# Layer A's first projections in a written order on three engines

## The chip, the cores and the metric

The kernel runs on one core of a Trainium2 chip. The core has a matrix engine (TensorE, PE in the profile), a vector engine (VectorE, DVE), a scalar engine for activations (ScalarE, ACT), a general engine (GpSimd, POOL) and a queue engine (SyncE, SP); sixteen DMA engines move data between HBM and the on-chip memories. Each engine takes its instructions in the order in which the compiled program lists them and waits, where it must, on semaphores. The metric is the device time of one execution in microseconds (us); the median of several executions is given.

## The reference, cut to what matters

The program is a two-layer decoder trunk over 1024 tokens of width 1024: layer A with sparse attention (compressed blocks, selected blocks, a sliding window), layer B with dilated attention, each followed by a feed-forward part. The change lies in the first steps of layer A:

```
h    = rmsnorm(x, norm_mix[0])
proj = h @ w_in                                  # (1024, 2608)
q, kc, vc, ks, vs, kwn, vwn, gl = split(proj)    # 1024, then six of 256, then 48 gates
k_cmp = gelu(blocks(kc) + pe_k @ w1_k) @ w2_k    # compressed keys; the same for v
bias  = rel_bias[t5_bucket(distance)]            # added to every attention logit
```

All products are to float32 accuracy. The kernel splits both factors into a high and a low part of a reduced type and takes three products for each pair (high x high, high x low, low x high).

## The kernel before

The function `trunk` writes out the whole program. The first stage of layer A, inside `with ExitStack() as c:` from line 567, does the following.

*Normed tokens, turned.* `norm_to_hT` (lines 388 to 402) loads token tiles of 128 x 1024 (`nx`, four buffers), takes the row scale (`row_scale`: square with a sum and square root on ACT, reciprocal on VectorE), scales the rows (`nxn`, line 395), turns 128 x 128 squares on PE against an identity (line 400) and splits the result into `hH` (ACT, line 351) and `hL` (VectorE, line 352), eight tiles each of 128 x 1024 tokens. It is called for token tiles 0 and 1, then 2 and 3, then 4 to 7. The products themselves are issued by `mm3`, lines 375 to 377.

*Compressed-key columns.* `proj_T` multiplies two weight column blocks (128 columns each, `blocks_weights`) with groups of tokens. `evac_c` copies the result into `kc2` by ACT (line 577) and, shifted by one token, by VectorE (lines 579 and 581).

*Bias rows.* `bias_rows` (lines 451 to 463) multiplies the bias table `rb` (33 x 16) with a onehot matrix (33 x 1917) in four products of up to 512 columns (line 461), copies them to `R` (line 462) and stores `R` to memory as `sR`. Later, `bias_skewed` copies it eight times, two heads at a time, with 128 shifted rows, into `sA` (line 472), from where the attention reads its bias. Each copy is issued by SP behind the newest weight load at that place.

*Values and gates.* `tok_proj` (line 418) with 304 columns gives the window values and the gates: for each of the eight token tiles, 24 products. `evac_v` (line 668) splits the values into `vt` (two buffers), stores them from POOL (line 672) and copies the gates (line 674).

*Behind it* come the compression, the second values, the compressed-value columns and the keys and queries, all with the same helpers, up to the attention, whose order is planned by the class `Order`.

Weights come through the class `Weights`: three raw buffers (`wraw`), five high (`wh`) and five low ones (`wl`), used in turn; a load is one DMA of SP and one split. Six PSUM banks named `mm` are shared by transposes, bias products, block columns and values, in the order in which the program asks for them.

What sets the order: except in the attention parts, where `Order` links instructions by hand, a compile-time scheduler lists the instructions of each engine; it takes the program's order as priority and, by a simulated time line, lets a later instruction go first where an earlier one isn't ready. SP's DMA issues are ordered in the same way. In the trace the values' weight splits, for example, stand between the norms and the splits of the first tokens.

Of the kernel before, what the change touches and what calls it, by code (L numbers as in the profile page):

```python
# [11 lines left out]
F32 = mybir.dt.float32  # L12
# [9 lines left out]
D = 1024  # L22
NT = S // 128
KC = D // 128
H = 16
# [89 lines left out]
class Order:  # L115
# [88 lines left out]
    def done(self):  # L204
# [75 lines left out]
        queued = mybir.DependencyInfo(mybir.DependencyClass.NoSync, mybir.DependencyReason.DATA)  # L280
        for e, row in order.items():
            if e == "SP":
                continue
            for a, b in zip(row, row[1:]):
                self.tc.add_manual_dep(b, a.name, queued, reason="order")
# [14 lines left out]
def trunk(ctx, tc, I, out):  # L300
# [33 lines left out]
    nc.vector.memset(eps, 1e-6)  # L334

    def gain(name, ap):
        t = cst.tile([128, KC], F32, name=name)
        nc.gpsimd.dma_start(t, ap.rearrange("(k p) -> p k", p=128))
# [15 lines left out]
    class Weights:  # L354
# [6 lines left out]
        def load(self, src, a, n, gains=None):  # L361
            raw, wh, wl = (r.tile() for r in self.rings)
            v = lambda t: t[:, :a * n].rearrange("p (a n) -> p a n", n=n)
            self.last = nc.sync.dma_start(v(raw), src.rearrange("(a p) n -> p a n", p=128))
            if gains is not None:
                nc.gpsimd.tensor_mul(v(raw), v(raw), gains.unsqueeze(2).to_broadcast([128, a, n]))
            split(wh[:, :a * n], wl[:, :a * n], raw[:, :a * n])
            return v(wh), v(wl)
# [19 lines left out]
    def norm_to_hT(p, xget, gains, hH, hL, t0, n):  # L388

        xs = []  # L390
        for t in range(t0, t0 + n):
            xt = xget(t)
            xn = p.tile([128, D], F32, name="nxn", bufs=4)
            rs = row_scale(p, xt, xn)
            nc.vector.tensor_scalar(xn, xt, rs, None, op0=OP.mult)
            xs.append(xn)
        for k in range(KC):
            pt = bank("mm")
            for i in range(n):
                nc.tensor.transpose(pt[:, i * 128:(i + 1) * 128], xs[i][:, k * 128:(k + 1) * 128], ident)  # L400
            tk = slice(t0 * 128, (t0 + n) * 128)
            split(hH[k][:, tk], hL[k][:, tk], pt[:, :n * 128], gains[:, k:k + 1])
# [15 lines left out]
    def tok_proj(ws, n, hT, tokens, evac):  # L418

        hH, hL = hT  # L420
        for t in range(NT):
# [29 lines left out]
    def bias_rows(p):  # L451
        rb = p.tile([33, H], F32, name="rb")
        nc.vector.memset(rb, 1.0)
        nc.gpsimd.dma_start(rb[0:32], I["rel_bias"])
        R = p.tile([H, NL], F32, name="R")
        for lo in range(0, NL, 512):
            n = min(512, NL - lo)
            oh = p.tile([33, 512], F32, name="oh", bufs=2)
            nc.gpsimd.dma_start(oh[:, :n], I["onehot"][:, lo:lo + n])
            ps = bank("mm")  # L460
            nc.tensor.matmul(ps[:H, :n], rb, oh[:, :n], start=True, stop=True)
            nc.vector.tensor_copy(R[:, lo:lo + n], ps[:H, :n])
        nc.gpsimd.dma_start(sR, R)
# [103 lines left out]
    with ExitStack() as c:  # L567
        wts = Weights([(pool(c, "pw", "right"), (3, 5, 5))])
        cctx = ExitStack()
# [22 lines left out]

        with ExitStack() as c2:
# [8 lines left out]
            kc2, ws = None, []  # L602
            for t0, n in ((0, 2), (2, 2), (4, 4)):
                norm_to_hT(np_, xget, g_mix[0], *hT, t0, n)
                if t0 < 4:
                    ws.append(blocks_weights(0, len(ws)))
                if t0 == 0:
                    kc2 = blocks_tile()
                done = t0 * 128, (t0 + n) * 128
                if t0 == 2:  # L610
                    proj_T(ws[0], hT, evac_c(kc2, 0), (done,))
                    proj_T(ws[1], hT, evac_c(kc2, 1), ((0, 512),))
                else:
                    for ch in range(len(ws)):
                        proj_T(ws[ch], hT, evac_c(kc2, ch), (done,))
        cp = pool(cctx, "pc")
        st = pool(c, "pst", "right")
# [50 lines left out]
        def evac_v(i):  # L668
            def f(t, ps):
                vt = st.tile([128, G, 128], F32R, name="vt", bufs=2)  # L670
                split(vt[:, :, 0:64], vt[:, :, 64:128], ps[:, :256].rearrange("p (g d) -> p g d", d=64))
                nc.gpsimd.dma_start(vS[i, t], f32(vt))
                if i == 1:
                    nc.vector.tensor_copy(gates[:, t, :], ps[:, 256:304])
            return f

        bias_rows(cp)
        tok_proj(wide(wts, W[:, 2304:2608], 304, 3), 304, hT, natural, evac_v(1))
# [24 lines left out]
        def store_blockind():  # L703
            for a in range(2):
                cols = slice(a * 512, (a + 1) * 512)
                raw = st.tile([16, 512], F32, name="bif", bufs=1)
                nc.gpsimd.dma_start(raw, I["blockind"][:, cols])
                t = st.tile([128, 512], F32R, name="sth", bufs=2)
# [1260 lines left out]
```

## Time and profile before

| | us |
|---|---|
| median of 3 runs | 2913.47 |
| lowest, highest | 2911.92, 2920.52 |
| the profiled execution | 2908.86 |
| its span in the profile | 2907.1 |
| first instruction of PE | 8.14 |
| last product of the values and gates ends | 86.44, where the first product of the compression follows |

The profile comes from one execution. Its span runs from the first to the last instruction; 1.8 us of the execution's time lie around it. Times in the text are from the span's start. A line such as "L400" is a line of the kernel before. In a group of instructions "x12" counts them, and "[3.35 <-DVE hL L352]" is idle time of the engine ahead of it, with what ended it. "PEclk" is the share of TensorE's full clock that was granted.

### The profile page before, as it was taken

What the parts mean: (1) busy time and instruction counts of PE and PEld (TensorE: products, weight loads), DVE (VectorE), ACT (ScalarE), POOL (GpSimd) and SP (SyncE); (2) the same over time, 40 slices, a digit from 0 to 9 for tenths busy, and PEclk for the clock granted to TensorE, in tenths of its full rate; (3) what the DMA queues carried; (4) which work ended last, traced back from release to release, by engine and by line L of the source; (5) the groups of instructions that cost most, each with busy time, mean ns of one, the idle gap of its engine ahead of it and who ended that gap; (6) DMA issues with size and microseconds to landing.
All of it is one profiled execution on the core that took longest, in us unless ns stands there. A gap on an engine that the chain in (4) does not pass through costs nothing.

```text
span 2907.1 us, 43848 instructions
## 1 busy us (share of the span) xinstructions
PE 2817.1 (97%) x14766; PEld 2371.2 (82%) x14766; DVE 2260.1 (78%) x4465; ACT 1522.0 (52%) x3314; POOL 1541.3 (53%) x1776
## 2 busy tenths in 40 slices
PE   7999999999999999999999999899999999999997
PEld 6988899898878888888777788788877788888885
DVE  5441999997488888988876776698965888888887
ACT  5431888886443333333554444689855433333334
POOL 2134877873165555555447786455522655555551
PEclk9999999999999999999999999999999999999999
DMA  6756243203122322231225555976421211111112
GB/s 167 232 159 190 64 111 89 62 24 117 30 70 68 80 62 66 66 80 51 92 86 161 150 161 159 281 200 187 135 88 37 75 60 52 55 54 59 52 44 76
DMA packets 266833, 294.46 MB, mean 101 GB/s; under 512 B 18099, under 2 KB 209475, under 8 KB 266608
## 3 DMA queue, kind: packets, MB, share of 16 engines
q1 hardware_dynamic: 246960, 231.50, 27.4%
q0 software_dynamic: 19648, 60.16, 6.8%
q8 instruction: 117, 1.92, 0.3%
q14 instruction: 108, 0.88, 0.1%
HBM read 228.49 MB, written 78.81 MB: 106 GB/s over the span
## 4 chain that ended last, share of the span: by engine, by line
PE 70%; DVE 16%; ACT 4%; issue 4%; DMA 3%; POOL 3%; SPq 1%; DVEq 0%; ACTq 0%; POOLq 0%
PE ux L375 5%; PE ux L376 5%; PE ux L377 5%; PE pt L485 5%; DVE pl L1003 5%; PE uy L375 4%; PE uy L376 4%; DVE xr L1061 4%; PE uy L377 4%; PE dx L376 3%; PE dx L377 3%; PE dr L375 3%; PE dx L375 3%; PE mm L375 3%; PE dr L376 3%
## 5 line engine op out<-in xcount | busy, mean ns | idle before, releaser
L1003 DVE TENSOR_TENSOR pl<-oT,ph 128x512 fp32r<-128x512 f32 x325 | 324.1, 1018 | 71.2 <-ACT ph L1002 61.9
L1002 ACT ACTIVATE ph<-oT 128x512 fp32r<-128x512 f32 x325 | 196.3, 626 | 214.0 <-PE ux L376 58.1
L485 PE MATMUL pt<-ident,P 128*128 128x128 f32 x1536 | 259.7, 277 | 4.5 <-DVE tl L349 2.6
L1003 DVE TENSOR_TENSOR pl<-oTb,ph 128x512 fp32r<-128x512 f32 x235 | 217.7, 951 | 50.6 <-ACT ph L1002 42.3
L1002 ACT ACTIVATE ph<-oTb 128x512 fp32r<-128x512 f32 x235 | 140.4, 625 | 177.0 <-PE ux L376 52.4
L1061 DVE TENSOR_TENSOR xr<-xr,dr 128x512 f32<-128x512 f32 x320 | 204.5, 678 | 27.6 <-PE dr L377 27.6
L1386 POOL TENSOR_TENSOR oT<-oT,gffn 128x512 f32<-128x512 f32 x92 | 108.7, 1188 | 208.6 <-DMA oT<-in_ffn_w_up_dram 184.0
L349 DVE TENSOR_TENSOR tl<-pt,th 128x512 fp32r<-128x512 f32 (+1 forms) x320 | 194.1, 624 | 19.4 <-ACT th L348 15.6
L485 PEld LDWEIGHTS pt<-ident,P 128*128 128x128 f32 x1536 | 181.2, 141 | 27.5 <-POOL P L924 3.4
L924 POOL TENSOR_SCALAR P<-P,sm,gates 128x384 f32<-128x384 f32 (+7 forms) x256 | 183.7, 730 | 37.4 <-DVE sm L922 31.7
L1061 DVE TENSOR_TENSOR xr<-xr,dx 128x512 f32<-128x512 f32 x320 | 199.9, 677 | 2.5 <-PE dx L377 1.8
L348 ACT ACTIVATE th<-pt 128x512 fp32r<-128x512 f32 (+1 forms) x320 | 168.4, 546 | 40.3 <-PE pt L485 30.8
L1386 POOL TENSOR_TENSOR oTb<-oTb,gffn 128x512 f32<-128x512 f32 x92 | 104.4, 1144 | 155.8 <-DMA oTb<-in_ffn_w_up_dram 129.5
L920 ACT ACTIVATE P<-P,m 128x384 f32<-128x384 f32 (+7 forms) x256 | 171.1, 671 | 12.5 <-DVE m L918 9.0
L376 PE MATMUL dx<-pl,ph 128*128 128x512 f32 x384 | 151.6, 395 | 0.9
L377 PE MATMUL dx<-ph,pl 128*128 128x512 f32 x384 | 149.0, 390 | 0.4 <-DVE pl L1003 0.4
L1760 ACT ACTIVATE P<-P,st 128x384 f32<-128x384 f32 (+2 forms) x256 | 139.5, 548 | 6.9 <-DVE st L1755 6.0
L510 PE MATMUL o<-tl,V 128*128 128x256 f32 x476 | 136.0, 303 | 0.0
L509 PE MATMUL o<-th,V 128*128 128x256 f32 x476 | 135.3, 299 | 0.2 <-DVE oTb L522 0.2
L1755 DVE CUSTOM_DVE_ANT_0 P<-s,T 128x384 f32<-128x384 f32 (+2 forms) x256 | 115.7, 478 | 16.1 <-PE s L1796 4.9
L375 PE MATMUL dx<-ph 128*128 128x512 f32 x384 | 116.9, 395 | 4.0 <-DVE xr L1503 2.1
L1002 ACT ACTIVATE ph<-wd 128x512 fp32r<-128x512 f32 x86 | 53.7, 629 | 115.0 <-PE ux L376 55.1
(922 smaller groups left out, 9481.3 us busy)
## 6 DMA issues: line engine op xcount, KB each, us to landing
qB<-xr POOLq DMA_DIRECT2D x96, 256.0 KB, 4.9
oT<-in_ffn_w_up_dram SPq DMA_DIRECT2D x92, 256.0 KB, 3.0
oTb<-in_ffn_w_up_dram SPq DMA_DIRECT2D x92, 256.0 KB, 3.0
Q<-qB SPq DMA_DIRECT2D x40, 512.0 KB, 7.1
wd<-in_ffn_w_down_dram SPq DMA_DIRECT2D x66, 256.0 KB, 2.6
oT<-in_b_w_q_dram SPq DMA_DIRECT2D x48, 256.0 KB, 3.4
K<-kBs SPq DMA_DIRECT2D x40, 256.0 KB, 9.5
wraw<-in_a_w_in_dram SPq DMA_DIRECT2D x18, 512.0 KB, 4.9
```

The costliest lines, as they stand in the source:

```text
L348: nc.scalar.activation(H_, src, AF.Copy)
L349: nc.vector.tensor_sub(L_, src, f32(H_))
L375: nc.tensor.matmul(ps, lh, rh, start=first, stop=False, skip_group_check=bool(shared))
L376: nc.tensor.matmul(ps, lh, rl, start=False, stop=False, skip_group_check=bool(shared))
L377: return nc.tensor.matmul(ps, ll, rh, start=False, stop=last, skip_group_check=bool(shared))
L485: nc.tensor.transpose(ps[:, i * 128:(i + 1) * 128], b, ident)
L920: nc.scalar.activation(P[:, e, :n], P[:, e, :n], AF.Exp, bias=mm[:, e:e + 1], scale=-1.0, accum_out=sm[:, e:e + 1])
L924: nc.gpsimd.tensor_scalar(P[:, e, :n], P[:, e, :n], sm[:, e:e + 1], gt(g, t, br, 2 * hp + e, 1), op0=OP.mult, op1=OP.mult)
L1002: nc.scalar.activation(like(h), src, AF.Copy)
L1003: (eng or nc.vector).tensor_sub(like(l), src, f32(like(h)))
L1061: nc.vector.tensor_add(xs, xs, banks[t])
L1386: nc.gpsimd.tensor_mul(v, v, gains[:, k:k + 4].unsqueeze(2).to_broadcast([128, 4, 128]))
```

## The change

The stage up to the last transposes is written out in the order in which three engines are to run it, and the order is fixed: each instruction of PE, ACT and VectorE that is traced between `start` and the loop's end is linked to the one before it on its engine (`in_turn`, taken out of `Order.done`). SP and POOL get no links, and instructions traced outside may be listed between linked ones.

- The four bias products and their copies come first, between the norms of the first two token tiles. The onehot matrix is one load of SP, `rb` stays a load of POOL, and `sR` is stored right behind.
- The gains other than layer A's first are loaded behind `rb`. A square root on one element ahead of everything fixes the table that ACT loads first.
- The first block column's weights are loaded and split in two parts. The values' weights are loaded in the stage too: the first of three loads through the weight buffers, the other two into `nx` buffers, between token tiles 1 and 2.
- Block columns and values follow each group of tokens: tokens 0 and 1, block columns, values; then tokens 2 and 3, block columns; then the values of tile 2, half of the transposes of tiles 4 to 7, the values of tile 3, the other half. Block columns and values of tiles 4 to 7 come behind the linked part.
- Transposes go by token tile first, in halves of four column blocks (`turn_rows`); one evacuation of values is put behind the first half of the next splits (`late`).
- `store_blockind` moves into the linked part; `evac_v` and the pool `pst` move up.

```diff
+def in_turn(tc, rows):
+    queued = mybir.DependencyInfo(mybir.DependencyClass.NoSync, mybir.DependencyReason.DATA)
+    for row in rows:
+        for a, b in zip(row, row[1:]):
+            tc.add_manual_dep(b, a.name, queued, reason="order")
...
+    nc.scalar.activation(cst.tile([128, 1], F32, name="first"), eps, AF.Sqrt)
 
     def gain(name, ap):
         t = cst.tile([128, KC], F32, name=name)
-        nc.gpsimd.dma_start(t, ap.rearrange("(k p) -> p k", p=128))
+        to_load.append(lambda: nc.gpsimd.dma_start(t, ap.rearrange("(k p) -> p k", p=128)))
         return t
 
+    to_load = []
     g_mix = [gain(f"gmix{i}", I["norm_mix"][i]) for i in range(2)]
+    to_load.pop(0)()
...
-        def load(self, src, a, n, gains=None):
-            raw, wh, wl = (r.tile() for r in self.rings)
+        def load(self, src, a, n, gains=None, parts=None, other=None):
+            raw, wh, wl = [other() if other and r is self.rings[0] else r.tile() for r in self.rings]
             v = lambda t: t[:, :a * n].rearrange("p (a n) -> p a n", n=n)
-            self.last = nc.sync.dma_start(v(raw), src.rearrange("(a p) n -> p a n", p=128))
+            cuts = [slice(i * a // (parts or 1), (i + 1) * a // (parts or 1)) for i in range(parts or 1)]
+            rows = src.rearrange("(a p) n -> p a n", p=128)
+            for c in cuts:
+                self.last = nc.sync.dma_start(v(raw)[:, c], rows[:, c])
...
+            fill = lambda c: split(*(t[:, c.start * n:c.stop * n] for t in (wh, wl, raw)))
+            if parts:
+                return (v(wh), v(wl)), [lambda c=c: fill(c) for c in cuts]
+            fill(cuts[0])
...
+    def turn_rows(xs, gains, hH, hL, t0, ks):
+
+        pts = [bank("mm") for _ in ks]
+        for i, xn in enumerate(xs):
+            for k, pt in zip(ks, pts):
+                nc.tensor.transpose(pt[:, i * 128:(i + 1) * 128], xn[:, k * 128:(k + 1) * 128], ident)
+        tk = slice(t0 * 128, (t0 + len(xs)) * 128)
+        return [lambda k=k, pt=pt: split(hH[k][:, tk], hL[k][:, tk], pt[:, :len(xs) * 128], gains[:, k:k + 1])
+                for k, pt in zip(ks, pts)]
...
     def bias_rows(p):
+
         rb = p.tile([33, H], F32, name="rb")
-        nc.vector.memset(rb, 1.0)
+        nc.gpsimd.memset(rb[32:33], 1.0)
         nc.gpsimd.dma_start(rb[0:32], I["rel_bias"])
         R = p.tile([H, NL], F32, name="R")
-        for lo in range(0, NL, 512):
+        oh = p.tile([33, NL], F32, name="oh")
+        nc.sync.dma_start(oh, I["onehot"])
+
+        def part(lo):
             n = min(512, NL - lo)
-            oh = p.tile([33, 512], F32, name="oh", bufs=2)
-            nc.gpsimd.dma_start(oh[:, :n], I["onehot"][:, lo:lo + n])
-            ps = bank("mm")
-            nc.tensor.matmul(ps[:H, :n], rb, oh[:, :n], start=True, stop=True)
-            nc.vector.tensor_copy(R[:, lo:lo + n], ps[:H, :n])
-        nc.gpsimd.dma_start(sR, R)
+            ps = bank("mm")[:H, :n]
+            nc.tensor.matmul(ps, rb, oh[:, lo:lo + n], start=True, stop=True)
+            return lambda: nc.vector.tensor_copy(R[:, lo:lo + n], ps)
+
+        return [lambda lo=lo: part(lo) for lo in range(0, NL, 512)], lambda: nc.gpsimd.dma_start(sR, R)
...
-            kc2, ws = None, []
-            for t0, n in ((0, 2), (2, 2), (4, 4)):
-                norm_to_hT(np_, xget, g_mix[0], *hT, t0, n)
...
+            start = len(nc.cur_bb.bb.instructions)
+            xs = [xget(0)]
+            parts, keep_rows = bias_rows(np_)
+            xs.append(xget(1))
+            for f in to_load:
+                f()
+            cols = lambda ch: W[:, 1024 + 128 * ch:1152 + 128 * ch]
+            ws = [wts.load(cols(ch), KC, 128, None, 2 - ch) for ch in range(2)]
+            wv = [wts.load(W[k * 128:min(k + 3, KC) * 128, 2304:2608], min(3, KC - k), 304, None, 1,
+                           k and (lambda: np_.tile([128, D], F32, name="nx", bufs=4))) for k in (0, 3, 6)]
+            xs += [xget(t) for t in range(2, 8)]
+            fills = [f for _, fs in ws + wv for f in fs]
...
+            xn, copies = [], [f() for f in parts]
+            for t in range(2):
+                copies[2 * t]()
+                xn.append(normed(np_, xs[t]))
+                copies[2 * t + 1]()
+            fs = turned(xn, 0, 0, 4)
+            run(fills[:1] + fs + fills[1:2])
+            run(turned(xn, 0, 4, 8))
+            run([copies[4] if len(copies) > 4 else lambda: None, keep_rows])
+            run(fills[2:3])
+            blocks(0, 2, 0)
+            run(fills[3:])
+            blocks(0, 2, 1)
+            xn = [normed(np_, xs[t]) for t in (2, 3)]
+            values(0)
+            late = []
+            values(1, late)
+            for ks in ((0, 4), (4, 8)):
+                run(turned(xn, 2, *ks) + late)
+                late = []
+            xn = [normed(np_, xs[t]) for t in (4, 5)]
+            blocks(2, 2, 0)
+            xn += [normed(np_, xs[t]) for t in (6, 7)]
+            blocks(2, 2, 1)
+            store_blockind()
+            values(2)
+            run(turned(xn, 4, 0, 4))
+            values(3)
+            run(turned(xn, 4, 4, 8))
+            rows = {}
+            for i in nc.cur_bb.bb.instructions[start:]:
+                if not type(i).__name__.startswith("Bass"):
+                    rows.setdefault(str(i.engine).split(".")[-1], []).append(i)
+            in_turn(tc, [rows[e] for e in ("PE", "Activation", "DVE")])
+            blocks(4, 4, 0, 1)
+            for t in range(4, 8):
+                values(t)
...
-        bias_rows(cp)
-        tok_proj(wide(wts, W[:, 2304:2608], 304, 3), 304, hT, natural, evac_v(1))
```

More of the change, by code (lines that the diff above doesn't have):

```diff
@@ L386, in row_scale, with normed @@
         return rs
[L388 to L402, printed above, removed]
+    def normed(p, xt):
+        xn = p.tile([128, D], F32, name="nxn", bufs=4)
+        rs = row_scale(p, xt, xn)
+        nc.vector.tensor_scalar(xn, xt, rs, None, op0=OP.mult)
+        return xn
+    def turn_rows(xs, gains, hH, hL, t0, ks):
[6 more added lines that the diff above has]
+                for k, pt in zip(ks, pts)]
     def alloc_hT(p):
@@ L416, in proj_T, with tok_proj @@
             evac(ps, tk)
-    def tok_proj(ws, n, hT, tokens, evac):
+    def tok_proj(ws, n, hT, tokens, evac, ts=range(NT)):
         hH, hL = hT
-        for t in range(NT):
+        for t in ts:
             ps = bank("mm")
@@ L568, in trunk @@
         wts = Weights([(pool(c, "pw", "right"), (3, 5, 5))])
+        st = pool(c, "pst", "right")
         cctx = ExitStack()
@@ L591, in blocks_weights, with evac_v, f, store_blockind @@
             return wts.load(W[:, c0:c0 + 128], KC, 128)
+        def evac_v(i):
+            def f(t, ps):
+                vt = st.tile([128, G, 128], F32R, name="vt", bufs=2)
+                split(vt[:, :, 0:64], vt[:, :, 64:128], ps[:, :256].rearrange("p (g d) -> p g d", d=64))
+                nc.gpsimd.dma_start(vS[i, t], f32(vt))
+                if i == 1:
+                    nc.vector.tensor_copy(gates[:, t, :], ps[:, 256:304])
+            return f
+        def store_blockind():
+            for a in range(2):
+                cols = slice(a * 512, (a + 1) * 512)
+                raw = st.tile([16, 512], F32, name="bif", bufs=1)
+                nc.gpsimd.dma_start(raw, I["blockind"][:, cols])
+                t = st.tile([128, 512], F32R, name="sth", bufs=2)
+                nc.scalar.copy(t[:16], raw)
+                nc.gpsimd.dma_start(bS[:, cols], f32(t[:16]))
         with ExitStack() as c2:
@@ L599, in xget @@
                 return xt
-            kc2, ws = None, []
-            for t0, n in ((0, 2), (2, 2), (4, 4)):
-                norm_to_hT(np_, xget, g_mix[0], *hT, t0, n)
[L605 to L615, printed above, removed]
+            start = len(nc.cur_bb.bb.instructions)
@@ new lines, in trunk, with run, blocks @@
+            xs += [xget(t) for t in range(2, 8)]
+            fills = [f for _, fs in ws + wv for f in fs]
+            ws = [w for w, _ in ws]
+            wv = [(wh[:, i], wl[:, i]) for (wh, wl), _ in wv for i in range(wh.shape[1])]
+            kc2 = blocks_tile()
+            turned = lambda xn, t0, *ks: turn_rows(xn, g_mix[0], *hT, t0, range(*ks))
+            def run(fs):
+                for f in fs:
+                    f()
+            def blocks(t0, n, *chs):
+                for ch in chs:
+                    proj_T(ws[ch], hT, evac_c(kc2, ch), ((t0 * 128, (t0 + n) * 128),))
@@ new lines, in values @@
+            def values(t, late=None):
+                ev = evac_v(1)
+                tok_proj(wv, 304, hT, natural, ev if late is None else lambda *a: late.append(lambda: ev(*a)), (t,))
+            xn, copies = [], [f() for f in parts]
[6 more added lines that the diff above has]
+            run(turned(xn, 0, 4, 8))
@@ L701, in evac_k @@
             return f
[L703 to L708, printed above, removed]
-                nc.scalar.copy(t[:16], raw)
-                nc.gpsimd.dma_start(bS[:, cols], f32(t[:16]))
         def evac_q(ch):
```

18 lines of the change are left out of this document (1 added, 17 removed).

## The prediction

> **What bounds the kernel now.** I read first the page's summary of engines, then busy time by stretch, cut where PE's (TensorE's) work in layer A's first stage changes kind.
>
> ```profile
> span 2907.1 us, 43848 instructions
> PE 2817.1 (97%) x14766; PEld 2371.2 (82%) x14766; DVE 2260.1 (78%) x4465; ACT 1522.0 (52%) x3314; POOL 1541.3 (53%) x1776
> ```
> ```profile
> core 0: us, PE busy (x) PEld busy (x) DVE busy (x) ACT busy (x) POOL busy (x), PEclk, DMA share, GB/s
> 0.00:8.14 8.14, 0.00 (x0) 0.00 (x0) 0.98 (x3) 5.04 (x7) 5.97 (x12) 1.00 0.80 225
> 8.14:27.19 19.05, 10.97 (x56) 8.95 (x56) 14.04 (x28) 16.18 (x38) 1.52 (x2) 0.93 0.97 296
> 27.19:52.90 25.71, 25.63 (x129) 21.44 (x129) 14.42 (x26) 12.04 (x25) 7.87 (x11) 0.92 0.24 50
> 52.90:58.18 5.28, 3.54 (x10) 0.67 (x9) 4.09 (x6) 2.34 (x4) 1.08 (x2) 1.00 0.62 181
> 58.18:86.44 28.26, 28.26 (x192) 28.26 (x193) 7.37 (x20) 6.04 (x12) 4.35 (x8) 0.94 0.58 161
> 86.44:287.40 200.96, 200.96 (x1084) 174.33 (x1082) 71.02 (x98) 68.72 (x103) 57.54 (x115) 1.00 0.69 199
> ```
> PE is the bound nearly everywhere, so an edit is worth what it takes from PE's empty or slow time. In this stage that time lies in three places: 8 us before the first instruction, 8 us idle in the second row, 1.7 us idle in the fourth. Next I read who is waited for, up to 86.5 us.
>
> ```profile
> PE mm L400 <- DVE nxn L395: 9.4, 2, 8.1
> PE mm L400 <- DVE hL L352: 6.2, 2, 3.4
> PE mm L461 <- DMA oh<-in_onehot_dram: 1.7, 1, 1.7
> ACT vt L348 <- DMA vS<-vt: 13.4, 4, 8.2
> ```
> The transposes (L400) wait for normed rows and for banks that the splits have not emptied; the bias products (L461) wait for a load. The last wait cost PE nothing, since the stretch around it (58.18 to 86.44) is full. From 86.44 to 287.40 PE is full at clock 1.00 with DMA at 0.69, so that stretch should start earlier by whatever this stage gives up.
>
> PE's rates come from stretches that hold only one kind of product.
>
> ```profile
> 28.00:30.00 2.00, 2.00 (x11) 0.50 0.13 31
> 42.00:52.00 10.00, 10.00 (x45) 1.00 0.17 17
> 70.00:80.00 10.00, 10.00 (x73) 1.00 0.67 196
> 58.20:61.70 3.50, 3.50 (x15) 0.54 0.45 97
> 17.50:18.40 0.90, 0.90 (x9) 1.00 1.01 403
> ...
> 37.41 4.31 PE L400 MATMUL mm<-ident,nxn 128*128 128x128 f32 x32
> ...
> 52.90 1.89 PE L461 MATMUL mm<-oh,rb 33*16 33x512 f32 x4
> 56.52 1.66 PE L461 MATMUL mm<-oh,rb 33*16 33x512 f32 x4 [1.74 <-DMA oh<-in_onehot_dram]
> ```
> At clock 1.00 a product of 512 columns takes 10.00/45 = 0.22 us, one of 304 takes 10.00/73 = 0.137, one of 256 about 0.11 (0.9/9, plus its edge), a transpose 4.31/32 = 0.135. At 0.50 one of 256 takes about 0.2. The bias products are eight instructions, 1.89 + 1.66 = 3.55 us. PE's work in the stage is 64 x 0.135 = 8.6, plus 21.8 for block columns (96 instructions of 512 columns' worth, at 0.225 with edges), plus 192 x 0.137 = 26.3 for values, plus 3.55: **60.3 us**. It occupies 8.14 to 86.44, 78.3 us; 18 us are idle or at half clock.
>
> **The change, part by part.** The amount of PE work stays. What changes is when it can run, so I follow the written order.
>
> ```profile
> 1.98 1.81 POOL L338 DMA_DIRECT2D gmix<-in_norm_mix_dram  x2
> ...
> 5.52 1.28 ACT L384 ACT_TABLE_LOAD   x1
> 7.01 1.04 ACT L382 ACTIVATE nxn<-nx 128x1024 f32<-128x1024 f32 x1
> 7.14 0.16 DVE L385 RECIPROCAL nrs<-nrs 128x1 f32<-128x1 f32 x1 [6.28 <-ACT nrs L384]
> ...
> 8.70 0.75 DVE L395 TENSOR_SCALAR nxn<-nx,nrs 128x1024 f32<-128x1024 f32 x1
> ...
> 12.32 1.06 ACT L382 ACTIVATE nxn<-nx 128x1024 f32<-128x1024 f32 x1 [2.27 <-DMA nx<-in_x_dram]
> 13.38 2.28 ACT L351 ACTIVATE hH<-mm,gmix 128x256 fp32r<-128x256 f32 x6
> ...
> 18.22 1.23 DVE L349 TENSOR_TENSOR wl<-wraw,wh 128x1024 fp32r<-128x1024 f32 x1 [0.46 <-ACT wh L348]
> ...
> 21.52 0.60 ACT L709 CAST sth<-bif 16x512 fp32r<-16x512 f32 x1
> ...
> 22.43 0.42 DVE L579 COPY kc<-mm 64x255 f32<-64x255 f32 x1 [0.71 <-ACT kc L577]
> ...
> 24.84 1.25 DVE L352 SCALAR_TENSOR_TENSOR hL<-mm,gmix,hH 128x256 fp32r<-128x256 f32 x3
> ...
> 53.96 0.68 DVE L462 COPY R<-mm 16x512 f32<-16x512 f32 x1 [1.10 <-PE mm L461]
> ...
> 59.39 0.52 POOL L463 DMA_DIRECT2D sR<-R  x1 [3.77 <-DVE R L462]
> ```
> ```profile
> sA<-sR SPq DMA_DIRECT2D x3, 1151.0 KB, 10.0
> ...
> gmix<-in_norm_mix_dram POOLq DMA_DIRECT2D x2, 4.0 KB, 6.8
> ...
> rb<-in_rel_bias_dram POOLq DMA_DIRECT2D x1, 2.0 KB, 3.3
> ```
> 1. **Bias first.** The products now wait for the small load rb, issued from POOL behind ident and the first gain, at about 3.0 us (the first gain is issued from 1.98, 0.9 us each). How long it takes to land there is unknown. Below: 3.3 us, its own row, when the DMA engines were half empty: 6.3 us. Above: 6.8 us, the gains' row in the same queue at the same moment, with DMA at 0.80: about 9.8. I take **9.5**, near the second, because the place and the load are the same. The onehot load, second on SP's queue, stands ahead of the second x tile, whose square began at 7.01 before; it isn't last.
>
> 2. **Products at a cold clock.** After 27.19 the granted clock was 0.50, after 58.18 it was 0.54, and each time it took some 3.5 to 4 us of work to come up. So 4 us at half rate do 2 us of work, the other 1.55 run at full rate: the four products end at 11.4, 13.3, 14.2 and 15.05. If nothing of this lifts the clock, they take 7.1 us instead of 5.55.
>
> 3. **Vector work, in its new order.** Copy (0.68) 12.1, reciprocal and scaling (0.16 + 0.75) 13.0; copy 14.0; copy 14.9; second row tile 15.8; last, shorter copy 16.3. Before, the second row tile was scaled at 9.45: 6.4 us earlier. But before it helped little: ACT (ScalarE) stood at the third x tile until 12.32 and began splitting only at 13.38. The Sqrt table load taken off the start (1.28 us) brings nothing here, because the bias products are later than the square roots. It would count only if rb came by about 6.
>
> 4. **First tokens.** Transposes of the second tile end at 16.4. VectorE then does half a weight split (about 0.62), four hL at 0.42, the other half, four more: 16.9, 18.6, 19.2, 20.9; then the second weights (1.23): 22.1. The first block column's 24 products follow it at half clock and end at 22.1; the second's run to 24.9 at full rate.
>
> 5. **Values.** Their weights are split behind the first column's copies (two of 0.42), ending at about 25.0, 26.1, 26.9. The first token tile's products end near 28.3, the second's at 28.3 + 24 x 0.137 = 31.6. They cover the norms of tiles 2 and 3.
>
> 6. **Tokens 2 and 3.** 16 transposes (2.16) to 33.8; pacing by splits and the delayed evacuation 0.6; 48 products of 256 columns (5.5) to 39.9.
>
> 7. **The rest is dense.** Values 3.3 (43.2), transposes 2.16 (45.4), values 3.3 (48.7), transposes 2.16 (50.8), 48 products of 512 columns 10.9 (61.7), four value tiles 13.3: 75.0. The two ACT casts of blockind (0.60 each) move from the start to a place covered by 3.3 us of values. Hand-offs at eight turns, some 0.17 us each, add 1.4: **76.4 against 86.44, 10.0 us less.**
>
> What had to be late elsewhere: the raw value weights now borrow x buffers, so x tiles 2 and 3 wait for the first two to be scaled (13.0, 15.8), and tiles 4 and 5 for the value splits (26 to 27). The loads ahead of tile 2 are 3.6 MB; 225 GB/s to 8.14 and 296 after bring them by 14. Tiles 4 to 7 are 2.1 MB, 7 us at that rate: by about 34, and ACT reaches their squares at about 36. sR's store moves from 59 us to about 17 on POOL's queue, where nothing urgent stands behind it. Widening the onehot tile and the earlier store pool cost SBUF alone. The other gains are covered until the feed-forward part.
>
> A rule of the Trainium skill (TensorE: Matmul & The Clock Gate, Part 4) says that transposes don't count as activity for the clock gate. By it the transposes in step 4 would stay at half rate. The trace differs at least for keeping the clock: 32 transposes alone (37.41, 4.31 us) ran at full rate, and the stretch behind them, 42 to 52, shows 1.00.
>
> **The rivals.**
> - *Cold head.* The opening work has gaps, and the 33-row products may not lift the clock; for it speaks 0.54 right after them at 58.2, against it that they had followed 1.74 us of idling. Price: 1.55 us in step 2, 16 x 0.105 = 1.7 in step 4, of which 1 shows, and a later start of full rate, 1: gain 6.5, 2907 us by the median. By the skill's rule above this would be the likelier course. A late rb (11 us) gives the same.
> - *Early rb.* At 6.3 the whole head moves by 3.2, gain 13 us, 2900.5. Against it speaks the gains' 6.8 us.
> - *Given back.* The compile-time scheduler still orders the 200 us behind the stage and all of SP's issues. PE there is full, so it can't do better, only worse; a gain given back leaves about 2911.
> - *Slower: x tiles behind the bias copies.* The first copy sA<-sR, issued at 62.13 before, becomes possible at about 20, ahead of x tiles 4 to 7 in SP's queue. The row below shows two issued together; the copies' median landing of 10.0 us and the 8.2 us that ACT then waited for a store behind them put one between 4 and 10 us, and I take 6.5, near the middle.
>
> ```profile
> 62.13 1.28 SPq L472 DMA_DIRECT2D sA<-sR  x2
> ```
> With one copy ahead, tile 7 still lands by about 36 to 40. From about 41 on each us delays the last transposes, which now stand in PE's fixed order ahead of everything else. At 51 the gain is gone, at 60 (four copies ahead) it is 9 us slower, 2922. Against it: later copies wait for weight loads whose buffers come free only after 55.
> - *The order isn't kept.* The links cover PE, ACT and VectorE alone; if they did nothing, the scheduler would run its own order and the moved bias alone would save 1.7 idle and 1.7 cold us of the two rows at 52.90 and 58.20: 2910.
>
> **How the numbers follow.** The profiled execution took 2908.86 us, of which 2907.1 is the span; 10.0 less is 2898.9. The median of the three runs was 2913.47, 4.6 above the profiled one, so by the median I predict **2903.5**. About 0.3%, 8.7 us, is what a measurement of this kernel can tell from no change. Forecast (gain 8.7 to 12.5) 0.45; early rb (over 12.5) 0.18; cold head or late rb (3 to 8.7) 0.20; given back or order not kept 0.12; slower 0.05. So faster 0.63, same 0.32, slower 0.05. The range 2897 to 2911 takes in the early rb, the cold head and part of the gain given back.
>
> **What would show it.** Bias products starting between 9 and 10 us and ending near 15; the first block product near 18; no PE idle over 1 us after 25; clock 1.00 from 22 on; the last value product near 76; and the end of the full stretch, now 287.40, earlier by the same 10 us. The forecast is wrong if rb lands at 6 or after 11, if PE waits for nx loads behind sA<-sR between 40 and 50, or if the stretch behind the stage is longer than 201 us.

## The result, and the profile after

| | before | after |
|---|---|---|
| median, us | 2912.69 | 2937.99 |
| lowest, highest | 2911.02, 2920.52 | 2935.76, 2947.96 |
| executions | 6 | 6 |
| profiled execution's span | 2907.1 | 2936.4 |

The changed kernel takes 1.0087 times the time of the kernel before, with an interval of 1.0075 to 1.01: 25 us more, where 10 us less had been forecast. Line numbers below are those of the kernel that a row comes from; the change and its variants moved many of them.

The page's summary of engines, after:

```profile
span 2936.4 us, 43891 instructions
PE 2855.4 (97%) x14790; PEld 2381.2 (81%) x14790; DVE 2253.1 (77%) x4467; ACT 1524.5 (52%) x3317; POOL 1527.4 (52%) x1773
```
PE (TensorE) is the only engine that is busier by much, 38 us more for 24 more rows. So look first for PE work that became slower, not for a wait.

**The stage itself** became shorter. PE's timeline after, at its start and at the first product behind it (start, duration, group):

```profile
9.76 6.55 PE L475 MATMUL mm<-oh,rb 33*16 33x512 f32 x8 [9.76 <-DMA rb<-in_rel_bias_dram]
16.23 3.77 PE L411 MATMUL mm<-ident,nxn 128*128 128x128 f32 x16
19.76 0.36 PE L386 MATMUL mm<-hH,wh 128*128 128x256 f32 x1
19.96 0.28 PE L387 MATMUL mm<-hL,wh 128*128 128x256 f32 x1
...
81.26 0.28 PE L386 MATMUL cmp<-bh,wh 128*128 128x256 f32 x1
```
The compression starts at 81.26, where before the values ended at 86.44: 5.2 us earlier. The table by stretch, in the same columns as before, shows in its second row where most of the rest of the forecast's 10 us went:

```profile
20.00:47.00 27.00, 25.79 (x200) 24.93 (x199) 18.92 (x41) 19.41 (x45) 1.15 (x2) 1.00 0.61 202
47.00:57.50 10.50, 8.32 (x46) 7.25 (x45) 4.37 (x10) 5.01 (x10) 4.31 (x7) 0.84 0.17 59
57.50:81.26 23.76, 23.76 (x143) 21.93 (x142) 11.70 (x20) 10.31 (x17) 5.69 (x9) 1.00 0.51 140
```
From 47 to 57.5 PE idles 2.2 us and the granted clock falls to 0.84. The timelines of ACT, POOL and PE there, one after the other:

```profile
46.76 0.60 ACT L624 CAST sth<-bif 16x512 fp32r<-16x512 f32 x1
50.24 0.62 ACT L624 CAST sth<-bif 16x512 fp32r<-16x512 f32 x1 [2.88 <-DMA bif<-in_blockind_dram]
```
```profile
47.65 0.51 POOL L625 DMA_DIRECT2D bS<-sth  x1 [10.48 <-ACT sth L624]
48.17 0.50 POOL L622 DMA_DIRECT2D bif<-in_blockind_dram  x1
```
```profile
51.98 0.30 PE L411 MATMUL mm<-ident,nxn 128*128 128x128 f32 x1 [0.94 <-DVE gates L615]
52.69 0.33 PE L411 MATMUL mm<-ident,nxn 128*128 128x128 f32 x1 [0.40 <-DVE hL L357]
```
`bif`, into which the rows of blockind are loaded, has one buffer. Its second load can be issued only when the first cast is done, and POOL issues it behind the first store, at 48.17. ACT stands 2.88 us at the second cast with the splits of the last tokens queued behind it, and the last transposes wait for banks that these splits and the values' evacuation have not emptied.

**At the attention's start** a wait appears that wasn't there. The rows of a tile give the smallest, median and largest duration in ns, then the first and the last start. The first scores, against the compressed keys, began at 287.2 before:

```profile
L836 PE MATMUL s<-kc,Q x256: 217/275/323, 287.2 to 656.8; 128*128 128x64 f32 x128
```
```profile
283.93 1.11 PE L900 MATMUL s<-kc,Q 128*128 128x64 f32 x8 [1.41 <-DVE stl L357]
```
```profile
285.00:290.00 5.00, 4.72 (x24) 4.52 (x24) 3.15 (x21) 2.31 (x11) 2.68 (x8) 0.57 0.51 137
```
After the change they begin at 283.93, behind 1.41 us of idling: 3.3 of the 5.2 us are left. Behind it the mean clock was 0.57 for 5 us; that is no fixed price of the wait, since e4 below has the same 1.41 us and shows 1.00 from 280 to 290. By the first product of the feed-forward part nothing is left of the gain against this profile of before (790.6 against 790.1). Three more profiles of before (e5, e16 and e17 below) reach that product at 792.7 to 794.3, so a part of this is chance. From there on the kernel only loses. The rows of the tile B11h, before and after:

```profile
L375 PE MATMUL ux<-B11h,ph x196: 389/389/504, 806.0 to 2836.9; 128*128 128x512 f32 x196
L375 PE MATMUL dx<-B11h,ph x16: 389/389/497, 790.1 to 2238.5; 128*128 128x512 f32 x16
```
```profile
L386 PE MATMUL ux<-B11h,ph x196: 391/396/497, 806.5 to 2866.1; 128*128 128x512 f32 x196
L386 PE MATMUL dx<-B11h,ph x16: 392/397/503, 790.6 to 2260.7; 128*128 128x512 f32 x16
```
The same products of the same shape take 396 instead of 389 ns at the median, and no longer 389 even at best. 500 us out of each layer's feed-forward part, before and after:

```profile
900.00:1400.00 500.00, 498.45 (x2168) 405.03 (x2167) 439.83 (x598) 189.47 (x326) 280.75 (x206) 1.00 0.25 65
2300.00:2800.00 500.00, 495.96 (x2150) 401.17 (x2150) 437.98 (x598) 188.69 (x325) 281.61 (x210) 1.00 0.18 56
```
```profile
900.00:1400.00 500.00, 499.10 (x2132) 398.65 (x2131) 429.18 (x585) 186.31 (x321) 271.25 (x205) 1.00 0.24 64
2300.00:2800.00 500.00, 498.56 (x2129) 398.03 (x2128) 427.52 (x584) 185.79 (x319) 277.62 (x209) 1.00 0.18 54
```
PE is nearly full in all four at clock 1.00, and a product costs 498.45 / 2168 = 229.9 ns of PE's time before and 499.10 / 2132 = 234.1 after in the first layer, 230.7 and 234.2 in the second. The feed-forward products run, before, from 790.1 to about 1497.9 (the row of transposes further down) and from 2238.5 to the end, 708 and 669 us. At the 4.34 and 4.30 products a us of before, 4.2 and 3.5 ns each come to some 13 + 10 = **23 us**, nearly the whole loss. This is an estimate from two stretches of 500 us.

The change touches none of these products. What it touches is where tiles lie: the square root's result, `first`, is a tile of one element in the pool of constants, which is laid out first. It takes 32 bytes of each partition. In the compiled programs' tables of addresses the tiles that stand on the left side of SBUF behind it start 32 bytes higher after, those of the feed-forward parts among them, while the tiles on the right side start where they did there. Two in three of the feed-forward products take one factor from each side. Before, the two starts were a multiple of 256 bytes apart in 8,704 of the 8,816 split products of 512 columns of the whole kernel. After, 5,208 of these, 4,368 of them into `ux` and `uy`, have factors that are 32 bytes off such a multiple.

### The profile page after: what moved, and what is told of

The parts are those of the page before. It is cut to its first block, busy times and chain, and to the rows that moved or that the text cites. A ratio compares the mean times of both kernels' runs of the same rounds, so it can differ in the third digit from the quotient of the medians.

```text
span 2936.4 us, 43891 instructions
## 1 busy us (share of the span) xinstructions
PE 2855.4 (97%) x14790; PEld 2381.2 (81%) x14790; DVE 2253.1 (77%) x4467; ACT 1524.5 (52%) x3317; POOL 1527.4 (52%) x1773
## 4 chain that ended last, share of the span: by engine, by line
PE 79%; DVE 10%; ACT 3%; issue 3%; POOL 2%; DMA 1%; SPq 0%; DVEq 0%; ACTq 0%; POOLq 0%
PE ux L386 6%; PE ux L387 6%; PE ux L388 6%; PE pt L500 5%; PE uy L386 5%; PE uy L387 5%; PE uy L388 5%; PE dx L387 4%; PE dx L388 4%; PE dr L386 4%; PE dx L386 3%; PE dr L388 3%; PE dr L387 3%; DVE pl L1067 3%; PE mm L386 2%
## 5 line engine op out<-in xcount | busy, mean ns | idle before, releaser
L1067 DVE TENSOR_TENSOR pl<-oT,ph 128x512 fp32r<-128x512 f32 x325 | 315.6, 992 | 77.7 <-ACT ph L1066 67.2
```

Of the source, the lines that this page charges most:

```text
L1067: (eng or nc.vector).tensor_sub(like(l), src, f32(like(h)))
```

## The experiments

Each kernel ran beside runs of the kernel before; the ratio is to those. "ux" is the median duration of `ux<-B11h,ph`, "first cmp" the start of the compression.

| run | edit | median us | ratio | ux ns | first cmp |
|---|---|---|---|---|---|
| e1 | before, 32 bytes on the left | 2935.19 | 1.0075 [1.0056, 1.0093] | 396 | 86.5 |
| e2 | after, right pad 32 bytes longer | 2934.85 | 1.0065 [1.0042, 1.0088] | 394 | |
| e3 | after without the tile | 2918.23 | 1.0014 [1.0005, 1.0024] | 389 | 80.6 |
| e4 | e3, two `bif` buffers | 2911.46 | 0.9991 [0.9982, 1.0] | 389 | 77.05 |
| e9 | before, 64 bytes on the left | 2936.04 | 1.0079 [1.0062, 1.0096] | 394 | 86.3 |
| e10 | before, both sides 32 bytes up | 2915.66 | 1.0005 [0.9994, 1.0017] | 389 | |
| e11 | before, 128 bytes on the left | 2932.77 | 1.0069 [1.0053, 1.0084] | 393 | |
| e15 | before, 256 bytes on the left | 2916.2 | 1.0002 [0.9991, 1.0014] | 389 | |
| e14 | after, both sides 32 bytes up | 2917.73 | 1.0013 [1.0004, 1.0022] | 390 | 81.7 |
| e6 | e4, five banks asked for | 2911.54 | 0.9986 [0.9977, 0.9995] | | 78.2 |
| e7 | e4, rb loaded first | 2907.58 | 0.9977 [0.9968, 0.9987] | 389 | 75.88 |
| e12 | e7, five banks written | 2908.36 | 0.9988 [0.9979, 0.9996] | | 75.9 |
| e13 | e7 without links | 2909.46 | 0.9988 [0.9979, 0.9997] | | 78.76 |

### Is it the tile, and what of it?

e1 adds to the kernel before nothing but an unused tile. The order of instructions on each engine stays as it was.

```diff
+    cst.tile([128, 1], F32, name="cell")
```


> The kernel before with one more tile of 128 x 1 in the constants' pool, which nothing writes or reads; no instruction is added or moved. It pushes every tile on the left side of the on-chip memory 32 bytes up, as the change's one-element square root does. Theory 'offset' (products whose two factors lie 32 bytes apart modulo 64 take about 7 ns longer each, some 5000 of them): 2938 to 2948 us, and the up-projection products ux and uy at a mean near 396 ns instead of 389. Theory 'order' (the loss behind the first stage comes from what the new order sets off later): no change, 2909 to 2917.

It costs 22.5 us, nearly the whole loss. e2 lengthens the pad that the kernel keeps at the start of the right side:

```diff
-    pool(ctx, "shift", "right").tile([128, 104], F32, name="shift")
+    pool(ctx, "shift", "right").tile([128, 112], F32, name="shift")
```


> The changed kernel with the pad tile on the right side 8 elements longer (112 instead of 104), so that the right side moves by 32 bytes too and both sides again agree modulo 64, though both now start at 32 modulo 64. Theory 'relative offset': the slow products go, 2903 to 2911 us. Theory 'absolute alignment' (a start off 64 bytes is slow for either factor): still 2935 or more, with the products of one pool (dx) slow too. Theory 'order': 2936 to 2940.

I read its loss at first as the fall of the distance between the sides and as support for a rule on each start by itself, 64 bytes. That was a mistake: the right side is laid out from the top down, so a longer pad moves its tiles down. e2 had taken the sides 64 bytes apart, as the addresses of its program show. e3 takes the tile out, with the square root written into the pad:

```diff
-    nc.scalar.activation(cst.tile([128, 1], F32, name="first"), eps, AF.Sqrt)
+    nc.scalar.activation(spare[:, 0:1], eps, AF.Sqrt)
```


> The changed kernel with the one-element square root written into the pad tile on the right side, so that no tile is added and all addresses of the later layers are those of the kernel before; order and instructions are the change's. Theory 'offset', relative or absolute: 2903 to 2911 us, products ux and uy back at 389 ns; first compression product near 81.3 us as in the changed kernel. Theory 'order': 2936 to 2940.

The products are back at 389 ns and 20 us are won back. The rows of e2 and e3:

```profile
L386 PE MATMUL ux<-B11h,ph x196: 388/394/501, 805.8 to 2864.1; 128*128 128x512 f32 x196
```
```profile
L386 PE MATMUL ux<-B11h,ph x196: 389/389/500, 803.6 to 2842.8; 128*128 128x512 f32 x196
```
e9 was to confirm the rule on 64 bytes, and felled it:

```diff
+    cst.tile([128, 16], F32, name="cell")
```


> The kernel before with an unused tile of 64 bytes per partition at the place where the 32-byte cell stood. Theory (a start 32 bytes off a multiple of 64 slows the products): nothing happens, products of 512 columns stay at 389 ns, time within 2 us of before, 2912.7. Rival (any shift against the padding that the right side was given costs): products at 394 to 397 ns and 2935, as with the 32-byte cell.

A start at a multiple of 64 loses as much as one between. e10, e11 and e15 set the distance against the start itself: e10 adds the tile of e1 and shortens the pad by as much (96 elements instead of 104), e11 adds 128 bytes on the left (a tile of 32 elements), e15 adds 256 (64 elements).

> The kernel before with the unused 32-byte cell on the left and a right-hand pad shorter by 32 bytes, so that tiles of both sides start 32 bytes higher and keep their distance. Theory R (what counts is the distance between the left and the right side's tiles: the version with both sides moved had moved them apart by 64, since the right side is laid out from the top down, and its products, 394 ns, are those of the 64-byte cell): products of 512 columns at 389 ns, time within 2 us of before. Theory A (each side's own address counts, and only the one of before is good): 394 to 397 ns and 2930 to 2937.

> The kernel before with an unused tile of 128 bytes on the left: left tiles start 128 bytes higher, right ones stay. Theory R with a period of 128 bytes or less, and theory A with such a period: products at 389 ns, time as before. Either theory with a longer period: 393 ns or more, and 2925 to 2937.

> The kernel before with an unused tile of 256 bytes on the left: left tiles move by 256 bytes against the right ones. If the rule repeats every 256 bytes: products at 389 ns and 2912 to 2915. If it reaches further: 392 ns or more and 2925 to 2937, as with 32, 64 and 128 bytes.

One row of the tile's view from each, in the order e1, e9, e11, e10, e15:

```profile
L376 PE MATMUL ux<-B11h,ph x196: 391/396/482, 807.9 to 2864.2; 128*128 128x512 f32 x196
```
```profile
L376 PE MATMUL ux<-B11h,ph x196: 388/394/502, 808.0 to 2860.9; 128*128 128x512 f32 x196
```
```profile
L376 PE MATMUL ux<-B11h,ph x196: 390/393/506, 807.5 to 2861.8; 128*128 128x512 f32 x196
```
```profile
L376 PE MATMUL ux<-B11h,ph x196: 389/389/628, 805.5 to 2838.5; 128*128 128x512 f32 x196
```
```profile
L376 PE MATMUL ux<-B11h,ph x196: 387/389/504, 807.6 to 2844.7; 128*128 128x512 f32 x196
```
The first three moved the sides apart by 32, 64 and 128 bytes and are slow; e10 moved both by 32 and e15 one side by 256, and they are as fast as before. So what counts is the distance, and 256 bytes are as good as none. A second sign: layer A's projections, both factors of which lie on the right, kept their 389 ns in the changed kernel (lines by form, 225 to 283 us):

```profile
L387 PE MATMUL mm<-hL,wh 128*128 128x512 f32 x85 | 33.1, 389 | 0.0
```
e14 is the changed kernel with the shorter pad alone, its tile kept:

> The changed kernel with the right-hand pad shorter by 32 bytes, its extra tile kept: left and right tiles are again as far apart as before the change. Theory (the distance alone costs the 23 us): products of 512 columns at 389 ns and 2918, as with the tile taken out. Rival (the tile or the square root costs in another way too): products at 389 ns, but a time above 2922.

```profile
L386 PE MATMUL ux<-B11h,ph x196: 388/390/560, 804.5 to 2844.7; 128*128 128x512 f32 x196
```
2917.73, as with the tile taken out: the distance is all that the tile costs, as far as these runs can tell. The Trainium skill (SBUF — State Buffer, "SBUF: two separate sides") says that among the engines only the port pair that VectorE and GpSimd share gives rise to contention. These runs show a cost of TensorE's products that depends on how far apart their two factors lie (396 against 389 ns); whether the two factors of a product disturb each other or one of them and a write was not tried.

### What the order itself gains

e4 gives `bif` a second buffer, so both loads are issued long before the casts.

```diff
-                raw = st.tile([16, 512], F32, name="bif", bufs=1)
+                raw = st.tile([16, 512], F32, name="bif", bufs=2)
```


> As the kernel before this one (square root in the pad tile), and two buffers instead of one for the raw blockind rows, so that the second cast no longer waits for its load. In the changed kernel ScalarE stood 2.9 us in that wait with the splits behind it. Theory 'cast on the path': the first compression product moves from 81.3 to 77 to 79 us, and the time falls by 2 to 4 us against the run before. Rival (the split chain is behind anyway): under 1 us.

Its stretch from 47 to 57.5 and its first compression product:

```profile
47.00:57.50 10.50, 10.27 (x65) 9.24 (x63) 6.86 (x13) 6.51 (x12) 6.45 (x9) 1.00 0.27 71
```
```profile
77.05 0.29 PE L386 MATMUL cmp<-bh,wh 128*128 128x256 f32 x1
```
The stall and the slow clock are gone and the stage ends at 77.05, 9.4 us before 86.44, and 3.6 before e3's 80.6. By the medians e4 is 6.8 us faster than e3, but the intervals of their ratios lie only 0.0005 apart, some 1.5 us, so 3.6 is not contradicted.

One profile of each doesn't give these times to a us. In four profiles of before the compression starts at 86.6, 86.9, 89.0 and 89.6, in four of e4 (e6, e18 and e19 below run the same program) at 77.05, 78.2, 77.5 and 77.7: 88.0 against 77.6 in the mean, **10.4 us**. e7 starts the bias products sooner:

```diff
-    nc.gpsimd.dma_start(ident, I["ident"])
...
-    to_load = []
+    to_load = [lambda: nc.gpsimd.dma_start(ident, I["ident"])]
...
-    to_load.pop(0)()
```


> The version without the extra tile and with two blockind buffers, and rb as the first load of POOL, ahead of ident and the first gain. Theory (rb's landing sets the head): bias products start at 5 to 8 instead of 9.8, and the first compression product comes as much earlier, up to 3 us: 74 to 76 instead of 77.0; time 2908 to 2911. Rival (ident and the gain behind it, or the second x tile, become the last): the bias products start early, but the first block product stays near 19.8 and the compression at 77.

```profile
7.96 6.54 PE L473 MATMUL mm<-oh,rb 33*16 33x512 f32 x8 [7.96 <-DMA rb<-in_rel_bias_dram]
14.43 4.13 PE L409 MATMUL mm<-ident,nxn 128*128 128x128 f32 x16
18.22 0.56 PE L384 MATMUL mm<-hH,wh 128*128 128x256 f32 x1
...
75.88 0.29 PE L384 MATMUL cmp<-bh,wh 128*128 128x256 f32 x1
```
Against e4's profile the products start 1.6 us earlier (7.96 against 9.58) and the stage ends 1.2 us earlier, which is no more than e4's four profiles differ by. Against their mean it is 1.7, and e12 below, with the same start, gives 75.9 too. This version has the lowest median, 0.9977 of before [0.9968, 0.9987]. e13 takes the links away:

```diff
-            in_turn(tc, [rows[e] for e in ("PE", "Activation", "DVE")])
```


> The version with rb first, without the links on PE, ACT and VectorE: the program's order is only the scheduler's priority. If the fixed order is needed: first compression product 2 to 8 us later than 75.9, time 2910 to 2915. If the order in which the program is written is enough: within 1 us of 75.9, and 2907.

```profile
L384 PE MATMUL cmp<-bh,wh x64: 274/282/287, 78.8 to 196.7; 128*128 128x256 f32 x64
```
The compression starts at 78.76, 2.9 us later than with links, in one profile. So most of the stage's gain is there without the links. Whether fixing the order is worth the rest isn't shown by the time: 0.9988 [0.9979, 0.9997] overlaps with e7's interval.

### The wait at the attention's start

The changed stage takes one bank more from the ring of six, since the first block columns run in one more piece. By the compiled program's table the last projection before the change lay on the sixth bank and now lies on the first, where the first scores go. e6 asks for five banks more.

```diff
+            bank("mm")
             for t in range(4, 8):
                 values(t)
+                bank("mm")
```


> The version without the extra tile and with two blockind buffers, and five banks of the ring of six asked for and left empty at the stage's end. Theory (the first scores of the attention fall on the bank of the last projection, because the change asks for one bank more than before): the wait of 1.41 us ahead of the first s<-kc product goes, as before the change, and the time falls by 1 to 2 us, to about 2910. Rival (the wait comes from something else that the change moved): the wait stays at 1.4 us and the time at 2911.5.

Nothing changed, and it could not have: a bank that nothing writes isn't laid out, so e6 is the program of e4 once more. e12 writes one element into each.

```diff
+            skip = lambda: nc.vector.memset(bank("mm")[0:1, 0:1], 0.0)
+            skip()
             for t in range(4, 8):
                 values(t)
+                skip()
```


> The version with rb first, and five banks of the ring of six really taken at the stage's end, each by a write of one element from VectorE (the banks left empty before had not been laid out at all, so that run was a second one of the same program). Theory (the first scores fall on the bank of the last projection): the last projection lies on the sixth bank, as before the change, the wait of 1.41 us ahead of the first s<-kc product goes, and the first one comes at 277 instead of 278.7; time 1 to 2 us lower than with rb first alone, about 2906. Rival: the wait stays, or five writes on VectorE cost as much in the stage.

The first scores and, by the rows of its tile, the selected-block scores in e7, then in e12:

```profile
278.74 0.99 PE L898 MATMUL s<-kc,Q 128*128 128x64 f32 x7 [1.41 <-DVE stl L355]
```
```profile
L974 PE MATMUL s<-K,QM x128: 277/393/481, 314.2 to 670.1; 80*128 80x512 f32 x80, 80*128 80x256 f32 x32, 80*128 80x384 f32 x16
```
```profile
277.16 1.00 PE L901 MATMUL s<-kc,Q 128*128 128x64 f32 x8
```
```profile
L977 PE MATMUL s<-K,QM x128: 279/393/481, 313.7 to 670.0; 80*128 80x512 f32 x80, 80*128 80x256 f32 x32, 80*128 80x384 f32 x16
```
The bank was the cause: the wait is gone and the start 1.6 us earlier. It is worth nothing: 0.5 us are left at the first selected-block score and 0.1 at the last, and the time is no lower than e7's (0.9988 against 0.9977).

### Where the rest of the gain goes

e4 reaches the first transposes of layer B's projections 7.3 us ahead of before, yet takes 0.9991 of its time [0.9982, 1.0]. Those transposes and the first query store behind them, before and in e4:

```profile
L1617 PE MATMUL dx<-ident,oT x24: 270/272/285, 1497.9 to 1570.5; 128*128 128x128 f32 x24
...
L1590 POOL DMA_DIRECT2D qB<-xr x96: 523/531/561, 1624.5 to 1836.4; - x96
```
```profile
L1681 PE MATMUL dx<-ident,oT x24: 270/272/285, 1490.6 to 1566.3; 128*128 128x128 f32 x24
...
L1654 POOL DMA_DIRECT2D qB<-xr x96: 526/533/561, 1626.8 to 1836.5; - x96
```
From the first transpose to the first store pass 126.6 us before and 136.2 in e4. e5, e16 and e17 profile the kernel before again, e18 and e19 profile e4 again, all without an edit.

> The kernel before once more, unchanged, for a second profile. The two versions without the misplaced tile gave back 8 to 10 us between 1500 and 1650 us of the span, in layer B's projections, where each engine's list is the same as before but for one pair of neighbours; the first profile of before shows no stretch of half clock there. Theory A (before's first profile was a lucky execution there): this profile is 3 to 10 us later by 1650 than the first, with one or more stretches of clock 0.50 between 1500 and 1650. Theory B (the change costs something there): this profile lies within 1 us of the first one at 1650, without half clock.

> The kernel before, a third profile. What layer B's projections (1500 to 1650 us of the first profile) cost here against the first profile: if the loss there is chance, 0 to 10 us, as wide as in the changed versions (5.7 to 10.3 so far); if the change brings it, 0 to 4.5 us as in the two profiles of before.

> The kernel before, a fourth profile; expected as for the third.

> The version without the extra tile and with two blockind buffers, a second profile (a third, with the one whose empty banks changed nothing; these two lost 10.3 and 8.9 us in layer B's projections against the first profile of before). If the loss is chance: some value between 0 and 10; if the change brings it: 8 to 11 again.

> The same version, one more profile; expected as for the one ahead of it.

This stretch took 126.6, 129.9, 130.0 and 132.3 us in the four profiles of before, 129.7 in the mean, and 136.2, 136.2 (e6, the same program), 135.1 and 138.1 in those of e4, 136.4 in the mean. Each theory had a part of it: chance moves the stretch by some 3 us either way, and 6.7 us come with the change. The other versions bear this out. With the old order of instructions it took 132.0 (e1), 130.9 (e9), 128.9 (e11), 127.2 (e10) and 129.5 (e15); with the new one 135.5 (the changed kernel), 137.6 (e2), 134.2 (e3), 137.0 (e14), 133.0 (e7), 137.5 (e12) and 136.4 (e13). All nine profiles of the old order lie below all eleven of the new one. Being early isn't the reason: the changed kernel and e2 reach the stretch at 1510.2 and 1506.4, later than before does, and lose as much.

The means of the four profiles of each, in us, show where the gain goes:

| | before | e4 | earlier by |
|---|---|---|---|
| first compression product | 88.0 | 77.6 | 10.4 |
| first scores against the compressed keys | 288.7 | 280.4 | 8.3 |
| first feed-forward product, layer A | 792.8 | 783.9 | 8.9 |
| first transposes of layer B's projections | 1500.9 | 1491.8 | 9.1 |
| first query store behind them | 1630.6 | 1628.2 | 2.4 |
| end of the span | 2912.8 | 2909.2 | 3.6 |

So about 9 of the 10.4 us come as far as layer B's projections, and most of the loss lies there. In that stretch PE idles 5.4 us in the mean of the four profiles of before and 9.1 in those of e4, and the mean granted clock is 0.97 to 1.00 against 0.96 to 0.97. The idle time is spread over several waits. What brings it stays open; no run tells it. The instructions and their buffers are the same there. What differs from before in the compiled lists of the new order (the changed kernel, e3, e4, e7, e12, e13 and e14 alike) is the order of a few neighbours on ACT and VectorE in the row norms of layer B ahead; in some, of a few on PE too. No run put the old order of these back, so they are a cause that was not tried.

The spans of the four profiles of before (2907.1, 2911.2, 2914.2, 2918.8) show besides that the first, from which the prediction was made, was the fastest of them.

## Why the prediction was wrong

**The step that failed** is its one sentence on memory, that widening the onehot tile and the earlier store pool "cost SBUF alone", together with the step on the table load, which asks only what the moved load saves and gives the tile of the square root's result no cost. For the two that it names the sentence holds (e3 keeps both, and its products take 389 ns); it leaves out the third, `first`. The list of what the change adds went through instructions, loads, waits and banks; it left out that a new tile in a pool that stands for the whole program moves every tile laid out behind it on the left side. The size of that term was 22.5 us (e1), more than twice the forecast gain. The five rivals all lay within the stage, its loads or the 200 us behind it; none could reach past 2922. This term alone doesn't explain why the forecast of 2903.5 was missed: without it e3 takes 2918.23, and e4 2911.46. Two more steps failed, in the stage and behind it, and the cause of the last is open.

**Right.** rb landed at 9.76, with 9.5 forecast from the gains' row. The order did what it says. The value weights in the x buffers and the one bias copy ahead of x tiles 4 to 7 cost nothing: no wait of PE for an x tile is in the trace, so the rival of the late x tiles fell. With the tile and the `bif` wait away, e4 ends the stage at 77.05 (77.6 in the mean of four profiles); 76.4 was forecast. The forecast of 10.0 us at the stage's end is thus met, by 9.4 in single profiles and 10.4 in the means.

**Right in sum, wrong in parts.** The bias products took 6.55 us, not 5.55, and the 16 transposes behind them 3.77 where 2.16 is the full rate: the cold-head rival, and the first block product came at 19.76 instead of near 18. Since e4 ends the stage only 0.65 late, the work behind it made most of that good. The Trainium skill's rule that transposes don't count for the clock gate (TensorE: Matmul & The Clock Gate, Part 4) fits their rate better than the forecast did, but not the second product behind them, which took 0.28 us at 19.96, as one of its shape does at clock 1.00 (81.26). The early-rb rival was as open as the forecast said, but with a smaller price: e7 loads rb first and gains 1.6 us at the start, not 3.2.

**Wrong in the stage.** The blockind casts were called "covered by 3.3 us of values". Their two instructions were; the second one's load, which one buffer held back until 48.17, was not. The sum has no term for this load. Its price is e3 against e4: 80.6 against 77.05, 3.6 us.

**Wrong behind the stage.** "That stretch should start earlier by whatever this stage gives up" held nearly to the last projection. Then the wait on the bank took some 2 us of it (5.2 to 3.3), most of which is lost a little further on without the wait too (e12), and layer B's projections took 6.7 of the 9.1 us that e4 still had. The rival "given back" spoke of the 200 us behind the stage; the losses came later, in stretches of which the prediction had read no row.

## What to carry to other kernels

A new tile is an edit to every tile laid out behind it on its side of SBUF: before such a change is priced, list the addresses before and after, and keep the distance between the two factors of the large products (here a multiple of 256 bytes). When PE is full at full clock in two profiles and one does fewer products in the same 500 us, compare the median of one shape of product before looking for a wait. A gain at the start of a kernel is worth what is left of it at the end, and a single profile of each kernel doesn't tell some 5 us of that from chance: four profiles of the kernel before span 11.7 us.

## What the runs showed of the hardware that was not expected

- Products of 512 columns in the feed-forward parts (`ux<-B11h,ph`) take 389 or 390 ns at the median when their factors' starts are a multiple of 256 bytes apart, and 393 to 396 when they are 32, 64 or 128 bytes off. The start itself doesn't count (e10). Other distances were not tried, and why it is so isn't known.
- The granted clock of a stretch doesn't tell everything. From 9.76 to 20.00 the profile of the changed kernel shows 1.00:

```profile
9.76:20.00 10.24, 10.22 (x26) 4.09 (x27) 6.63 (x14) 3.00 (x7) 0.51 (x1) 1.00 1.06 296
```
There eight products of 512 columns took 6.55 us, 0.82 each, where before four took 1.89 us at 52.90, 0.47 each; the 16 transposes behind them took 0.24 each, where 32 in a row took 0.135 each at 37.41 in the kernel before. Whether the clock was lower than recorded or something else slowed them isn't shown.
